# A decoder block's feed-forward stage: a fourth unit of seven block products, and weight sums moved to transfers within SBUF

## The chip, the cores and the metric

The kernel runs on one core of a Trainium2 chip. The metric is device time in microseconds of one execution. Three runs of the kernel before gave 487.75, 488.26 and 488.61 us (median 488.26). One more execution was profiled; all views below come from it.

## The reference, cut to what matters

A block of a decoder with 256 tokens and 1024 channels: a gated linear recurrence and a block attention in parallel, joined, projected, and then a dense feed-forward network (FFN). The change touches only the FFN:

```python
h2 = rmsnorm(x, ffn_norm_g[l])
x = x + (jax.nn.silu(h2 @ w_ffn_gate[l]) * (h2 @ w_ffn_up[l])) @ w_ffn_down[l]
```

`w_ffn_gate` and `w_ffn_up` are 1024 x 2816, `w_ffn_down` is 2816 x 1024, all float32.

## The kernel before, in words

**Precision by splits.** Every float32 operand of a matmul is split in two: a high half, rounded to the fp32r type by a copy on ScalarE (ACT), and a low half, the difference, by a subtraction on VectorE (DVE). A product is then three matmuls: high x high, high x low, low x high. So each 1 MB piece of weights (128 partitions x 2048 elements) costs one ACT cast (L793, `h:` in the order below), one DVE subtraction (L797, `l:`), and matmuls on TensorE (PE, `M:`). Raw weights, high halves and low halves have three buffers each.

**The FFN.** The 2816 columns are cut in three: the first 768 are computed as feature blocks (a, b, e, f: features on partitions, 256 tokens along the row), 1024 columns "B" and 1024 columns "A" as token blocks (tokens on partitions). Gate columns of B and A, and up columns of A, are each a *unit* of seven block products (`scheme`, L919): the product of a 2 x 2 block of tokens and channels by a 2 x 2 block of channels and columns takes seven block products in place of eight, at the price of sums of weight blocks and of token blocks beforehand and of result blocks afterwards. The units are GB, GA and UA. A unit loads four quarters w11, w21, w12, w22 of 1 MB (`L:GBw11` and so on), each into a tile of its own tag, and forms four weight sums in place: 5 (w11 with w12), 6 (w11 with w22), 7 (w12 with w22) and 4 (w21 with w11). A sum is a DVE addition (`S:`, L928) or a transfer that adds while it writes (`A:`, L933, issued by GpSimd, POOL). Product 1 uses w11 as loaded, so sum 5 may only be written once product 1's split has read w11; sum 6 follows the split of 5, and so on. `f:` folds a result block into another on DVE (L968), `c:` copies one from PSUM on ACT (L965), `s:` is the silu, `x:` the product of up and gate.

The up columns of B are computed plainly by `tok` (L971): four pieces v0 to v3, each 1 MB of weights and 24 matmuls of 512 columns. Results of B and A are transposed by PE (`turn`, L997, names `tB..`, `tA..`) and split, and eleven `down` steps (d0 to d10, L1034) of 24 matmuls each multiply them by `w_down` into four PSUM banks.

**The order.** Each step is a closure in a table `todo`; the list `ORDER` (L1069), which a planner has written, says in which order the closures are issued. Each engine works off its own instructions in that order: PE the `M:`, ACT `h: c: s: i:`, DVE `l: S: f: x: k:`, the SP queue the loads `L:`, POOL the `A:`. An instruction that has to wait holds up all behind it on its engine. `SEQ` (L1065) is PE's order in short, `BY_DMA` names the sums that go by transfer, `tags` gives the tiles of each unit's quarters, and `fixed` its PSUM banks. A tile with a tag is free again when the last reader of what was there is done.

Of the kernel before, what the change touches and what calls it, by code (L numbers as in the profile page):

```python
# [11 lines left out]
OP = mybir.AluOpType  # L12
AX = mybir.AxisListType

P = 128
S = 256
D = 1024
KT = D // P
# [9 lines left out]
def tile_hgrn2_moba_block(ctx: ExitStack, tc: tile.TileContext, xm, xw, table, runs,  # L28
                          w_in, w_hg, w_at, w_out, w_gate, w_up, w_down, out):
    nc = tc.nc  # L30
# [7 lines left out]
    def pw(name="pw"):  # L38
        return psum.tile([P, 512], F32, name=name, tag="pw", bufs=4)
# [11 lines left out]
    def part(pair, k, m):  # L51
        return pair[k // 4][:, k % 4, m, :]
# [83 lines left out]
    for kt in range(KT):  # L136
        n0 = 0 if kt == 0 else NV
        t = big.tile([P, NX + D - n0], F32, name=f"xw{kt}", tag=("T3", "T4", "T5", "T1", "T7", "T8", "T9", "T11")[kt])
# [29 lines left out]
    for kt in range(KT):  # L168
        i = kt % 2
# [34 lines left out]
    for j in range(7):  # L204
        c = 1 << j
        n = 64 // c
        for tb in range(2):
            m = mask[:, j, tb, :].rearrange("p (n c) -> p n c", c=c)
# [70 lines left out]
    for half in range(2):  # L279
        ps = F0 if half == 0 else feat_block(w_in, 1024 + half * 512, XT, cut=2 - half)  # L280
        for j in range(2):
            h = half * 4 + j * 2
# [44 lines left out]
    for half in range(2):  # L327
        ps = feat_block(w_in, half * 512, XT)
        for j in range(2):
            h = half * 4 + j * 2  # L330
# [7 lines left out]
    A = big.tile([P, 2, H, P], F32, name="A", tag="T5")  # L338
# [321 lines left out]
    turn_a, b1, turn_h, b3 = pa("turn"), pa("b1"), ph("turn"), ph("b3")  # L660
# [76 lines left out]
    for half in range(2):  # L737
        hs = slice(half * 512, (half + 1) * 512)
        ps = tok_block(w_hg, half * 512, oT)
        for tb in range(2):  # L740
# [6 lines left out]
            ts = slice(tb * P, (tb + 1) * P)  # L747
# [36 lines left out]
    def rows(w, k0, n, c0, cw):  # L784
        return w[k0 * P:(k0 + n) * P, c0:c0 + cw].rearrange("(k p) c -> p k c", p=P)

    todo = {}
# [13 lines left out]
    def chunk(name, src, shape):  # L801
        t = {}

        def load():
            t["raw"] = wp.tile([P] + shape, F32, name="wraw")
            nc.sync.dma_start(t["raw"], src)

        todo["L:" + name] = load
        halve(name, lambda: t["raw"], shape, t)
        return t  # L810
# [85 lines left out]
    class Unit:  # L896
# [13 lines left out]
        def src(self, ij):  # L910
            i, j = int(ij[0]) - 1, int(ij[1]) - 1
            return rows(self.weights, 4 * i, 4, self.c0 + j * 512, 512)
# [6 lines left out]
    def scheme(u):  # L919

        q, banks = u.q, {}

        def load(ij):
            u.w[ij] = big.tile([P, 4, 512], F32, name="W" + ij, tag=dict(zip(("11", "21", "12", "22"), tags[u.name]))[ij])
            nc.sync.dma_start(u.w[ij], u.src(ij))

        def plus(a, b):
            nc.vector.tensor_add(u.w[a], u.w[a], u.w[b])  # L928

        for ij in ("11", "21", "12", "22"):  # L930
            todo[f"L:{u.name}w{ij}"] = lambda ij=ij: load(ij)
        def onto(a, src):
            nc.gpsimd.dma_start(u.w[a], src(), accum_op=OP.add)  # L933

        for k, a, other in (("5", "11", "12"), ("6", "11", "22"), ("7", "12", "22"), ("4", "21", "11")):
            if u.name + k in BY_DMA:
                src = (lambda: u.w["11"][:]) if k == "4" else (lambda other=other: u.src(other))
                todo[f"A:{u.name}{k}"] = lambda a=a, src=src: onto(a, src)
            else:
                todo[f"S:{u.name}{k}"] = lambda a=a, other=other: plus(a, other)  # L940

        def mm(k, t):
            b = {"2": 1, "5": 2, "3": 2}.get(k, 0)
            if k in "125":
                banks[b] = late_bank(fixed[u.name][b]) if u.name in fixed else (pa, ph, pa)[b]()
            act = tokens(*{"1": (0, 0), "2": (0, 1), "4": (1, 1)}[k], x2T) if k in "124" else \
                summed({"5": 0, "6": 1, "7": 2, "3": 3}[k], sums2)
            product(banks[b], act, (t["hi"], t["lo"]), k in "125")

        def through(k, i, j):  # L950
            src = banks[0] if k == "4" else q(i, j)
            if u.gate is None:
                nc.scalar.activation(q(i, j), src, AF.Silu, scale=(r2, r2n)[j if k != "4" else 0][:, i:i + 1])
            elif k in "37":
                nc.vector.scalar_tensor_tensor(q(i, j), src, -1.0, u.gate.q(i, j), op0=OP.mult, op1=OP.mult)
            else:
                nc.vector.tensor_mul(q(i, j), src, u.gate.q(i, j))

        for k, ij in {"1": "11", "2": "21", "5": "11", "6": "11", "7": "12", "3": "22", "4": "21"}.items():
            t = {}  # L960
            name = u.name + k
            halve(name, lambda ij=ij: u.w[ij], [4, 512], t)
            todo["M:" + name] = lambda k=k, t=t: mm(k, t)
        for k, b, i, j in (("1", 0, 0, 0), ("5", 2, 1, 1), ("6", 0, 0, 1)):
            todo["c:" + u.name + k] = lambda b=b, i=i, j=j: nc.scalar.copy(q(i, j), banks[b])  # L965
        for k, b, i, j in (("2", 1, 0, 0), ("3", 2, 0, 1), ("7", 0, 1, 1), ("4", 0, 1, 0)):
            if k != "4":
                todo["f:" + u.name + k] = lambda b=b, i=i, j=j: nc.vector.tensor_add(q(i, j), q(i, j), banks[b])  # L968
            todo[("x:" if u.gate else "s:") + u.name + k] = lambda k=k, i=i, j=j: through(k, i, j)

    def tok(name, j, k0):  # L971

        t = chunk(name, rows(w_up, k0, 4, FB * P + j * 512, 512), [4, 512])
        u = units["UB"]

        def mm():
            if k0 == 0:
                u.ps[j] = [pw(), pw()]
            for i in range(4):
                for tb in range(2):  # L980
                    ts = slice(tb * P, (tb + 1) * P)
                    for m, w in ((0, t["hi"]), (0, t["lo"]), (1, t["hi"])):
                        nc.tensor.matmul(u.ps[j][tb], part(x2T, k0 + i, m)[:, ts], w[:, i, :],  # L983
                                         start=(k0 + i == 0 and m == 0 and w is t["hi"]),
                                         stop=(k0 + i == KT - 1 and m == 1))

        def take(i):
            nc.scalar.copy(u.q(i, j), u.ps[j][i])

        todo["M:" + name] = mm  # L990
        if k0:
            for i in range(2):
                todo[f"c:{name}{i}"] = lambda i=i: take(i)
                k = {(0, 0): "2", (0, 1): "3", (1, 1): "7", (1, 0): "4"}[i, j]
                todo["x:B" + k] = lambda i=i: nc.vector.tensor_mul(u.q(i, j), u.q(i, j), units["GB"].q(i, j))

    def turn(name):  # L997

# [35 lines left out]
    def down(n, f0):  # L1034
# [28 lines left out]
        todo["M:" + name] = mm  # L1063

    SEQ = """  # L1065
        a0 a1 GB1 b0 b1 GB2 e v0 v1 GB5 GB6 GB3 GB7 v2 GB4 v3 tB10 f d0 tB11 tB01 tB00 GA1 GA2 d1 GA5 d2 GA6
        GA3 GA7 d3 GA4 UA1 UA2 d4 UA5 d5 UA6 UA3 UA7 tA001 tA010 d6 tA110 UA4 d7 tA101 d8 d9 d10
    """.split()
    ORDER = """  # L1069
        L:b1 M:a0 L:GBw21 M:a1 L:e h:b0 C0 C1 L:GBw12 Ch0 l:b0 c:a10 h:b1 M:GB1 L:v0 f:a10 c:a11 f:a11 M:b0 h:GB2  # L1070
        L:GBw22 l:b1 s:a10 s:a11 c:GB1 l:GB2 L:v1 S:GB5 M:b1 h:e l:e A:GB7 Cl0 c:b10 L:v2 f:b10 M:GB2 h:v0 C3 c:b11
        l:v0 M:e h:v1 f:b11 L:v3 i:b10 l:v1 i:b11 C2 L:f M:v0 k:b10 h:GB5 k:b11 Ch1 l:GB5 c:e0 S:GB6 M:v1 Cl1 h:GB6
        f:e0 l:GB6 s:e0 M:GB5 h:GB3 S:GB4 c:v11 l:GB3 L:GAw21 M:GB6 h:GB7 c:GB5 l:GB7 M:GB3 L:GAw11 h:v2 c:GB6 l:v2
        M:GB7 h:GB4 L:GAw12 c:v10 l:GB4 M:v2 h:v3 L:d0 f:GB7 l:v3 s:GB7 L:GAw22 f:GB2 f:GB3 M:GB4 h:f L:d1 s:GB2 l:f
        M:v3 s:GB4 h:d0 x:B4 L:d2 s:GB3 l:d0 x:B2 L:d3 M:tB10 c:v30 M:f c:v31 i:tB10 x:B7 h:GA1 x:B3 k:tB10 l:GA1
        S:GA5 M:d0 c:f0 h:GA2 f:f0 A:GA7 l:GA2 i:f0 M:tB11 h:d1 k:f0 M:tB01 M:tB00 M:GA1 i:tB11 i:tB01 k:tB11 i:tB00
        l:d1 M:GA2 h:GA5 L:d4 c:GA1 l:GA5 M:d1 h:d2 l:d2 k:tB01 L:d5 S:GA6 M:GA5 S:GA4 h:GA6 M:d2 h:GA3 l:GA6
        L:UAw21 c:GA5 l:GA3 M:GA6 h:GA7 k:tB00 L:UAw11 f:GA2 s:GA2 l:GA7 M:GA3 h:d3 L:UAw12 c:GA6 l:d3 M:GA7 h:GA4
        L:d6 l:GA4 M:d3 h:UA1 f:GA7 L:UAw22 l:UA1 s:GA7 S:UA5 M:GA4 h:UA2 f:GA3 A:UA7 s:GA3 l:UA2 M:UA1 h:d4 s:GA4
        l:d4 M:UA2 h:UA5 L:d7 c:UA1 l:UA5 M:d4 h:d5 l:d5 S:UA6 L:d8 M:UA5 f:UA2 h:UA6 x:UA2 M:d5 c:UA5 l:UA6 h:UA3  # L1080
        l:UA3 S:UA4 M:UA6 h:UA7 l:UA7 M:UA3 h:d6 c:UA6 l:d6 M:UA7 h:UA4 f:UA3 L:d9 x:UA3 M:tA001 h:d7 f:UA7 M:tA010
        M:d6 x:UA7 l:UA4 i:tA010 i:tA001 k:tA010 k:tA001 l:d7 M:tA110 M:UA4 i:tA110 L:d10 h:d8 k:tA110 l:d8 M:d7
        h:d9 x:UA4 l:d9 M:tA101 M:d8 i:tA101 h:d10 k:tA101 l:d10 M:d9 M:d10
    """.split()
    BY_DMA = ("GA7", "GB7", "UA7")
    late, acc, units = {}, [], {}
    tags = {"GB": ("T10", "T9", "T11", "T8"), "GA": ("T8", "T10", "T11", "T9"), "UA": ("T9", "T8", "T11", "T10")}
    fixed = {"GA": (0, 1, 2), "UA": (3, 1, 2)}
    sums2 = token_sums2()
    for name in ("GB", "UB", "GA", "UA"):  # L1090
        units[name] = Unit(name)
# [70 lines left out]
```

## Time and profile before

| | us |
|---|---|
| median of three runs | 488.26 |
| profiled execution | 488.07 |
| its span, first to last instruction | 486.4 |
| PE busy | 481.6 |
| VectorE busy | 398.5 |
| ScalarE busy | 308.1 |
| GpSimd busy | 28.7 |
| FFN, from its first feature block (304.8) to the last matmul's end | 178 |

The granted TensorE clock was 0.999 of full speed over the span. In the rows of the profile an instruction is "line engine operation written<-read"; "x12" counts instructions, and in brackets stands the idle time ahead of the instruction with what ended it. PE's matmuls overlap, so their distance from start to start is what they cost, not their duration.

### The profile page before, as it was taken

What the parts mean: (1) busy time and instruction counts of PE and PEld (TensorE: products, weight loads), DVE (VectorE), ACT (ScalarE), POOL (GpSimd) and SP (SyncE); (2) the same over time, 40 slices, a digit from 0 to 9 for tenths busy, and PEclk for the clock granted to TensorE, in tenths of its full rate; (3) what the DMA queues carried; (4) which work ended last, traced back from release to release, by engine and by line L of the source; (5) the groups of instructions that cost most, each with busy time, mean ns of one, the idle gap of its engine ahead of it and who ended that gap; (6) DMA issues with size and microseconds to landing.
All of it is one profiled execution on the core that took longest, in us unless ns stands there. A gap on an engine that the chain in (4) does not pass through costs nothing.

```text
span 486.4 us, 6399 instructions
## 1 busy us (share of the span) xinstructions
PE 481.6 (99%) x2538; PEld 403.2 (83%) x2538; DVE 398.5 (82%) x406; ACT 308.1 (63%) x400; POOL 28.7 (6%) x62
## 2 busy tenths in 40 slices
PE   9999999999999999999999999999999999999997
PEld 7888888888888888988888888888878888888886
DVE  5769999697779979499987766889997889989853
ACT  5977646767758984876555445874686547656520
POOL 1930220000000000000000000001000100100000
PEclk9999999999999999999999999999999999999999
DMA  8977695724523348508247575778379466780402
GB/s 310 402 245 256 188 298 184 239 88 138 209 88 132 131 139 291 175 12 334 86 174 250 183 244 189 260 259 225 121 271 340 125 170 222 261 245 11 152 21 88
DMA packets 43695, 94.31 MB, mean 194 GB/s; under 512 B 1673, under 2 KB 3977, under 8 KB 43665
## 3 DMA queue, kind: packets, MB, share of 16 engines
q1 hardware_dynamic: 41344, 88.11, 52.2%
q0 software_dynamic: 2320, 5.79, 5.4%
q8 instruction: 20, 0.33, 0.3%
q14 instruction: 11, 0.08, 0.1%
HBM read 92.82 MB, written 1.07 MB: 193 GB/s over the span
## 4 chain that ended last, share of the span: by engine, by line
PE 94%; DVE 3%; issue 2%; ACT 1%; ACTq 0%
PE acc L1043 12%; PE pw L83 10%; PE pw L84 10%; PE pw L85 10%; PE late L642 8%; PE pw L101 6%; PE pw L165 5%; PE b L642 4%; PE pw L844 4%; PE pa L642 2%; PE pw L983 2%; DVE wlo L797 2%; PE pw L100 2%; PE pw L103 2%; PE pw L680 1%
## 5 line engine op out<-in xcount | busy, mean ns | idle before, releaser
L56 DVE TENSOR_TENSOR wlo<-wraw,whi 128x2048 fp32r<-128x2048 f32 (+1 forms) x42 | 91.5, 2187 | 23.0 <-ACT whi L55 22.8
L55 ACT CAST whi<-wraw 128x2048 fp32r<-128x2048 f32 (+1 forms) x42 | 76.6, 1831 | 38.1 <-PE pw L85 19.6
L83 PE MATMUL pw<-whi,XT 128*128 128x512 f32 x144 | 56.9, 395 | 0.0
L85 PE MATMUL pw<-whi,XT 128*128 128x512 f32 x144 | 56.2, 390 | 0.0
L84 PE MATMUL pw<-wlo,XT 128*128 128x512 f32 x144 | 56.1, 390 | 0.0
L797 DVE TENSOR_TENSOR wlo<-wraw,whi 128x2048 fp32r<-128x2048 f32 x21 | 48.1, 2289 | 9.8 <-ACT whi L793 9.6
L793 ACT CAST whi<-W 128x2048 fp32r<-128x2048 f32 x21 | 40.1, 1915 | 25.2 <-DVE W L928 13.1
L797 DVE TENSOR_TENSOR wlo<-W,whi 128x2048 fp32r<-128x2048 f32 x21 | 47.9, 2289 | 6.4 <-ACT whi L793 6.4
L793 ACT CAST whi<-wraw 128x2048 fp32r<-128x2048 f32 x21 | 40.2, 1912 | 19.8 <-PE pw L844 4.9
L101 PE MATMUL pw<-XT,whi 128*128 128x512 f32 x128 | 40.6, 395 | 0.0
L85 PEld LDWEIGHTS pw<-whi,XT 128*128 128x128 f32 x144 | 27.0, 188 | 5.7
L83 PEld LDWEIGHTS pw<-whi,XT 128*128 128x128 f32 x144 | 27.0, 188 | 5.6
L84 PEld LDWEIGHTS pw<-wlo,XT 128*128 128x128 f32 x144 | 27.1, 188 | 5.4
L844 PE MATMUL pw<-x2T,whi 128*128 128x512 f32 x96 | 31.3, 397 | 0.0
L1043 PE MATMUL acc<-whi,hq 128*128 128x512 f32 x92 | 29.1, 390 | 0.0
L928 DVE TENSOR_TENSOR W<-W,W 128x2048 f32<-128x2048 f32 x9 | 20.6, 2287 | 0.1
L1043 PEld LDWEIGHTS acc<-whi,hq 128*128 128x128 f32 x92 | 17.3, 188 | 3.6
L983 PE MATMUL pw<-whi,x2T 128*128 128x512 f32 x64 | 20.2, 389 | 0.0
L101 PEld LDWEIGHTS pw<-XT,whi 128*128 128x128 f32 x128 | 19.8, 189 | 0.2
L1043 PE MATMUL acc<-wlo,hq 128*128 128x512 f32 x46 | 17.9, 390 | 0.0
L100 PE MATMUL pw<-XT,wlo 128*128 128x256 f32 x64 | 17.8, 278 | 0.0
L103 PE MATMUL pw<-XT,wlo 128*128 128x256 f32 x64 | 17.8, 277 | 0.0
(372 smaller groups left out, 1136.7 us busy)
## 6 DMA issues: line engine op xcount, KB each, us to landing
wraw<-w_in SPq DMA_DIRECT2D x26, 1024.0 KB, 5.1
wraw<-w_down SPq DMA_DIRECT2D x11, 1024.0 KB, 5.0
W<-w_gate SPq DMA_DIRECT2D x8, 1024.0 KB, 7.0
wraw<-w_up SPq DMA_DIRECT2D x7, 1024.0 KB, 5.2
wraw<-w_at SPq DMA_DIRECT2D x4, 1024.0 KB, 6.2
W<-w_in SPq DMA_DIRECT2D x4, 1024.0 KB, 5.2
wraw<-w_hg SPq DMA_DIRECT2D x4, 1024.0 KB, 6.8
wraw<-w_out SPq DMA_DIRECT2D x4, 1024.0 KB, 5.3
```

Of the source, the lines that this page charges most:

```text
L55: high = nc.scalar.copy(hi, src)
L56: return high, nc.vector.tensor_sub(lo, src, hi.bitcast(F32))
L83: nc.tensor.matmul(ps[tb], part(act, kt, 0)[:, ts], wh, start=(kt == 0), stop=False)
L84: nc.tensor.matmul(ps[tb], part(act, kt, 0)[:, ts], wl, start=False, stop=False)
L85: nc.tensor.matmul(ps[tb], part(act, kt, 1)[:, ts], wh, start=False, stop=(kt == KT - 1))
L101: nc.tensor.matmul(ps[ct], hi[:, i, cs], both, start=(kt == 0), stop=(kt == KT - 1))
L642: mm = nc.tensor.matmul(bank, act(kt, m), h[:, kt, :], start=(first and kt == 0 and m == 0 and h is hi), stop=(kt == 3 and m == 1), skip_g ...
L793: nc.scalar.copy(t["hi"], raw())
L797: nc.vector.tensor_sub(t["lo"], raw(), t["hi"].bitcast(F32))
L844: nc.tensor.matmul(block["ps", up][ct], t["hi"][:, i, cs], both, start=(kt == 0), stop=(kt == KT - 1))
L983: nc.tensor.matmul(u.ps[j][tb], part(x2T, k0 + i, m)[:, ts], w[:, i, :], start=(k0 + i == 0 and m == 0 and w is t["hi"]), stop=(k0 + i == ...
L1043: nc.tensor.matmul(bank, ACTS[f0 + i](m, ts), w[:, i, c0:c0 + cw], start=(st and i == 0 and m == 0 and w is t["hi"]), stop=(en and i == 1 ...
```

## The change

The up columns of B become a fourth unit of seven products, UB; `tok` goes. Ten of the sixteen weight sums are made by transfers, and these now read the other quarter from SBUF, where the three of before read it from DRAM a second time. Before, the list of order, the tiles and the banks were made for three units; they are made anew. The order of the down steps' features is the same.

```diff
-        def onto(a, src):
-            nc.gpsimd.dma_start(u.w[a], src(), accum_op=OP.add)
...
             if u.name + k in BY_DMA:
-                src = (lambda: u.w["11"][:]) if k == "4" else (lambda other=other: u.src(other))
-                todo[f"A:{u.name}{k}"] = lambda a=a, src=src: onto(a, src)
+                todo[f"A:{u.name}{k}"] = lambda a=a, other=other: nc.gpsimd.dma_start(u.w[a], u.w[other], accum_op=OP.add)
...
-    def tok(name, j, k0):
...
     SEQ = """
-        a0 a1 GB1 b0 b1 GB2 e v0 v1 GB5 GB6 GB3 GB7 v2 GB4 v3 tB10 f d0 tB11 tB01 tB00 GA1 GA2 d1 GA5 d2 GA6
-        GA3 GA7 d3 GA4 UA1 UA2 d4 UA5 d5 UA6 UA3 UA7 tA001 tA010 d6 tA110 UA4 d7 tA101 d8 d9 d10
+        a0 a1 GB1 b0 GB2 b1 GB5 GB6 GB3 GB7 e GB4 f UB1 UB2 d0 UB5 UB6 UB3 UB7 d1 UB4 GA1 tB002 GA2 d2 GA5
+        GA6 tB101 GA3 GA7 d3 tB112 GA4 UA1 UA2 tB012 d4 d5 UA5 UA6 UA3 UA7 d6 tA011 tA113 UA4 tA002 d7 tA102
+        d8 d9 d10
     """.split()
     ORDER = """
...
+        L:GBw12 M:a0 L:GBw21 L:b1 L:e L:GBw22 M:a1 A:GB5 h:b0 C0 C1 Ch0 l:b0 c:a10 L:f h:GB2 M:GB1 f:a10 c:a11 l:GB2
+        s:a10 f:a11 M:b0 h:b1 C3 c:GB1 l:b1 s:a11 M:GB2 C2 h:GB5 L:d0 Cl0 A:GB7 Ch1 l:GB5 M:b1 S:GB6 Cl1 A:GB4 h:GB6
+        f:GB2 M:GB5 h:GB3 l:GB6 c:b10 l:GB3 M:GB6 h:GB7 c:GB5 l:GB7 L:UBw11 M:GB3 c:GB6 L:UBw21 h:e f:b10 L:UBw12
...
+        k:b10 c:e0 l:UB1 M:f h:UB2 f:e0 i:b11 s:GB4 S:UB5 s:e0 s:GB3 l:UB2 A:UB7 M:UB1 h:d0 k:b11 c:f0 l:d0 M:UB2
+        h:UB5 L:d3 c:UB1 l:UB5 M:d0 S:UB6 f:f0 A:UB4 h:UB6 f:UB2 M:UB5 h:UB3 l:UB6 i:f0 l:UB3 M:UB6 c:UB5 h:UB7
...
+        L:UAw11 M:tB101 h:d3 L:UAw21 M:GA3 L:UAw12 i:tB101 l:d3 c:GA6 M:GA7 h:GA4 k:tB101 L:d6 s:GA2 l:GA4 M:d3
+        h:UA1 f:GA7 L:UAw22 f:GA3 s:GA7 l:UA1 s:GA3 A:UA5 M:tB112 h:UA2 M:GA4 i:tB112 l:UA2 M:UA1 h:d4 k:tB112 s:GA4
+        l:d4 M:UA2 h:d5 L:d7 l:d5 M:tB012 M:d4 A:UA7 i:tB012 h:UA5 k:tB012 L:d8 c:UA1 l:UA5 S:UA6 M:d5 f:UA2 A:UA4
+        h:UA6 x:UA2 l:UA6 M:UA5 h:UA3 l:UA3 M:UA6 c:UA5 h:UA7 l:UA7 M:UA3 h:d6 c:UA6 l:d6 M:UA7 h:UA4 f:UA3 L:d9
...
     """.split()
-    BY_DMA = ("GA7", "GB7", "UA7")
+    BY_DMA = ("GA4", "GA7", "GB4", "GB5", "GB7", "UA4", "UA5", "UA7", "UB4", "UB7")
     late, acc, units = {}, [], {}
-    tags = {"GB": ("T10", "T9", "T11", "T8"), "GA": ("T8", "T10", "T11", "T9"), "UA": ("T9", "T8", "T11", "T10")}
-    fixed = {"GA": (0, 1, 2), "UA": (3, 1, 2)}
+    tags = {"GB": ("T10", "T9", "T11", "T8"), "UB": ("T8", "T10", "T11", "T9"),
+            "GA": ("T9", "T8", "T11", "T10"), "UA": ("T10", "T9", "T11", "T8")}
+    fixed = {"UB": (0, 1, 2), "GA": (3, 1, 2), "UA": (0, 1, 2)}
```

More of the change, by code (lines that the diff above doesn't have):

```diff
@@ L969, in scheme @@
             todo[("x:" if u.gate else "s:") + u.name + k] = lambda k=k, i=i, j=j: through(k, i, j)
-    def tok(name, j, k0):
[L973 to L995, printed above, removed]
     def turn(name):
@@ L1065, in tile_hgrn2_moba_block @@
     SEQ = """
-        a0 a1 GB1 b0 b1 GB2 e v0 v1 GB5 GB6 GB3 GB7 v2 GB4 v3 tB10 f d0 tB11 tB01 tB00 GA1 GA2 d1 GA5 d2 GA6
-        GA3 GA7 d3 GA4 UA1 UA2 d4 UA5 d5 UA6 UA3 UA7 tA001 tA010 d6 tA110 UA4 d7 tA101 d8 d9 d10
+        a0 a1 GB1 b0 GB2 b1 GB5 GB6 GB3 GB7 e GB4 f UB1 UB2 d0 UB5 UB6 UB3 UB7 d1 UB4 GA1 tB002 GA2 d2 GA5
+        GA6 tB101 GA3 GA7 d3 tB112 GA4 UA1 UA2 tB012 d4 d5 UA5 UA6 UA3 UA7 d6 tA011 tA113 UA4 tA002 d7 tA102
+        d8 d9 d10
     """.split()
     ORDER = """
-        L:b1 M:a0 L:GBw21 M:a1 L:e h:b0 C0 C1 L:GBw12 Ch0 l:b0 c:a10 h:b1 M:GB1 L:v0 f:a10 c:a11 f:a11 M:b0 h:GB2
@@ L1071, in tile_hgrn2_moba_block @@
[L1071 to L1080, printed above, removed]
@@ L1081, in tile_hgrn2_moba_block @@
-        l:UA3 S:UA4 M:UA6 h:UA7 l:UA7 M:UA3 h:d6 c:UA6 l:d6 M:UA7 h:UA4 f:UA3 L:d9 x:UA3 M:tA001 h:d7 f:UA7 M:tA010
-        M:d6 x:UA7 l:UA4 i:tA010 i:tA001 k:tA010 k:tA001 l:d7 M:tA110 M:UA4 i:tA110 L:d10 h:d8 k:tA110 l:d8 M:d7
-        h:d9 x:UA4 l:d9 M:tA101 M:d8 i:tA101 h:d10 k:tA101 l:d10 M:d9 M:d10
+        L:GBw12 M:a0 L:GBw21 L:b1 L:e L:GBw22 M:a1 A:GB5 h:b0 C0 C1 Ch0 l:b0 c:a10 L:f h:GB2 M:GB1 f:a10 c:a11 l:GB2
+        s:a10 f:a11 M:b0 h:b1 C3 c:GB1 l:b1 s:a11 M:GB2 C2 h:GB5 L:d0 Cl0 A:GB7 Ch1 l:GB5 M:b1 S:GB6 Cl1 A:GB4 h:GB6
@@ new lines, in tile_hgrn2_moba_block @@
+        f:GB2 M:GB5 h:GB3 l:GB6 c:b10 l:GB3 M:GB6 h:GB7 c:GB5 l:GB7 L:UBw11 M:GB3 c:GB6 L:UBw21 h:e f:b10 L:UBw12
+        c:b11 M:GB7 l:e h:GB4 i:b10 l:GB4 L:d1 M:e h:f f:GB7 s:GB2 L:UBw22 l:f s:GB7 f:b11 L:d2 M:GB4 h:UB1 f:GB3
+        k:b10 c:e0 l:UB1 M:f h:UB2 f:e0 i:b11 s:GB4 S:UB5 s:e0 s:GB3 l:UB2 A:UB7 M:UB1 h:d0 k:b11 c:f0 l:d0 M:UB2
+        h:UB5 L:d3 c:UB1 l:UB5 M:d0 S:UB6 f:f0 A:UB4 h:UB6 f:UB2 M:UB5 h:UB3 l:UB6 i:f0 l:UB3 M:UB6 c:UB5 h:UB7
+        L:GAw11 l:UB7 M:UB3 c:UB6 L:GAw21 h:d1 k:f0 L:GAw12 M:UB7 l:d1 h:UB4 l:UB4 L:d4 M:d1 h:GA1 f:UB7 L:GAw22
@@ new lines, in tile_hgrn2_moba_block @@
+        l:GA1 f:UB3 x:UB2 M:UB4 h:GA2 x:UB3 S:GA5 M:GA1 h:d2 l:GA2 A:GA7 l:d2 M:tB002 h:GA5 M:GA2 i:tB002 l:GA5 L:d5
+        M:d2 S:GA6 k:tB002 A:GA4 h:GA6 x:UB7 x:UB4 c:GA1 M:GA5 l:GA6 h:GA3 f:GA2 M:GA6 h:GA7 l:GA3 c:GA5 l:GA7
+        L:UAw11 M:tB101 h:d3 L:UAw21 M:GA3 L:UAw12 i:tB101 l:d3 c:GA6 M:GA7 h:GA4 k:tB101 L:d6 s:GA2 l:GA4 M:d3
+        h:UA1 f:GA7 L:UAw22 f:GA3 s:GA7 l:UA1 s:GA3 A:UA5 M:tB112 h:UA2 M:GA4 i:tB112 l:UA2 M:UA1 h:d4 k:tB112 s:GA4
+        l:d4 M:UA2 h:d5 L:d7 l:d5 M:tB012 M:d4 A:UA7 i:tB012 h:UA5 k:tB012 L:d8 c:UA1 l:UA5 S:UA6 M:d5 f:UA2 A:UA4
@@ L1084, in tile_hgrn2_moba_block @@
+        h:UA6 x:UA2 l:UA6 M:UA5 h:UA3 l:UA3 M:UA6 c:UA5 h:UA7 l:UA7 M:UA3 h:d6 c:UA6 l:d6 M:UA7 h:UA4 f:UA3 L:d9
+        x:UA3 M:d6 h:d7 f:UA7 x:UA7 l:UA4 l:d7 M:tA011 M:tA113 L:d10 i:tA011 M:UA4 i:tA113 k:tA011 h:d8 k:tA113
+        M:tA002 x:UA4 M:d7 i:tA002 h:d9 k:tA002 l:d8 l:d9 M:tA102 M:d8 i:tA102 h:d10 k:tA102 l:d10 M:d9 M:d10
     """.split()
-    BY_DMA = ("GA7", "GB7", "UA7")
+    BY_DMA = ("GA4", "GA7", "GB4", "GB5", "GB7", "UA4", "UA5", "UA7", "UB4", "UB7")
     late, acc, units = {}, [], {}
-    tags = {"GB": ("T10", "T9", "T11", "T8"), "GA": ("T8", "T10", "T11", "T9"), "UA": ("T9", "T8", "T11", "T10")}
```

## The prediction

> **What bounds the kernel now.** I read the page first, then the chain of waits from 300 us on, then the timelines of PE, DVE and POOL around its one hole, then the groups and the DMA rows.
>
> ```profile
> span 486.4 us, 6399 instructions
> PE 481.6 (99%) x2538; PEld 403.2 (83%) x2538; DVE 398.5 (82%) x406; ACT 308.1 (63%) x400; POOL 28.7 (6%) x62
> ...
> PE 94%; DVE 3%; issue 2%; ACT 1%; ACTq 0%
> ```
>
> The profiled execution took 488.07 us: 486.4 of span and 1.67 around it. PE carries 94% of the chain that ended last. A busy PE need not be at its peak, so the pitch of the matmuls matters:
>
> ```profile
> 307.77 0.47 PE pw L844 x2
> ...
> 308.47 0.47 PE pw L844 x2
> ...
> 317.42 2.72 PE pa L642 x12
> ...
> 362.12 5.44 PE pw L983 x24
> ```
>
> A step of the token products (L983, 24 matmuls) takes 5.44 us and a block product (L642, 12 matmuls) 2.72: both 0.227 us per matmul, without a gap. The feature blocks a, b, e, f repeat four matmuls (two wide, two half) every 0.70 us, so each of their 32-matmul steps takes 8 x 0.70 = 5.60. From 305 us on PE runs at these pitches but for one place:
>
> ```profile
> 355.74 0.47 PE L642 MATMUL pa<-whi,C2h 128*128 128x512 f32 x1
> 356.62 0.50 PE L642 MATMUL pa<-wlo,C2h 128*128 128x512 f32 x1 [0.41 <-DVE wlo L797]
> ...
> 361.96 0.39 PE L983 MATMUL pw<-whi,x2T 128*128 128x512 f32 x1
> ```
>
> At 355.74 product GB3 begins; 24 matmuls later (GB3, GB7) v2 should begin at 355.74 + 5.44 = 361.18 and begins at 361.96. The hole of 0.78 us is DVE's: GB3's low half came late. DVE at that place:
>
> ```profile
> 352.08 2.28 DVE L928 TENSOR_TENSOR W<-W,W 128x2048 f32<-128x2048 f32 x1
> 354.28 4.49 DVE L797 TENSOR_TENSOR wlo<-W,whi 128x2048 fp32r<-128x2048 f32 x2
> ```
>
> The weight sum S:GB4 (L928) stands right ahead of GB3's split (L797). So the FFN is PE's sum plus one DVE hole.
>
> **The change, part by part.**
>
> *The seven products.* v0 to v3 are 4 x 5.44 = 21.76 us of PE; UB's seven products are 7 x 2.72 = 19.04. PE does 2.72 us less. Transposes (four of B, four of A), the other products and the eleven downs are the same in number. All of it lies on PE, hence on the path: **-2.72**.
>
> *DVE and ACT.*
>
> ```profile
> L797 DVE TENSOR_TENSOR wlo<-W,whi 128x2048 fp32r<-128x2048 f32 x21 | 47.9, 2289 | 6.4 <-ACT whi L793 6.4
> L928 DVE TENSOR_TENSOR W<-W,W 128x2048 f32<-128x2048 f32 x9 | 20.6, 2287 | 0.1
> ...
> L968 DVE TENSOR_TENSOR q<-q,late 128x512 f32<-128x512 f32 x6 | 4.1, 681 | 0.0
> ```
>
> ```profile
> L793 ACT CAST whi<-W 128x2048 fp32r<-128x2048 f32 x21 | 40.1, 1915 | 25.2 <-DVE W L928 13.1
> ```
>
> ```profile
> 300.00:470.00 170.00, 169.59 (x811) 141.35 (x810) 146.83 (x115) 107.66 (x101) 3.93 (x3) 1.00 0.61 196
> ```
>
> Seven splits replace four: three more on DVE (3 x 2.29) and ACT (3 x 1.92). UB's three folds (as L968) add 3 x 0.68 on DVE. Each unit of seven products has four weight sums. Before, three units have twelve, three by transfer and nine on DVE; after, four units have sixteen, ten by transfer and six on DVE (GB6, UB5, UB6, GA5, GA6, UA6): -3 x 2.29. DVE comes out 6.87 + 2.04 - 6.87 = 2.0 us longer, 149 of about 167 us; ACT some 5 us longer, 113. Neither becomes the bound as a sum, so this is priced at nothing, covered by PE's 2.7 to 5.6 us steps. Where the cover is thin I follow the queue.
>
> *The hole at GB3.* S:GB4 leaves DVE and becomes a transfer. Rows for the small pieces, and the start of the queue:
>
> ```profile
> L825 DVE TENSOR_TENSOR C2l<-C,C2h 128x1024 fp32r<-128x1024 f32 x2 | 2.4, 1219 | 0.0
> ...
> L871 DVE TENSOR_TENSOR zt<-zt,R 128x512 f32<-128x512 f32 x3 | 2.1, 692 | 0.1
> ...
> L819 DVE TENSOR_TENSOR C<-x2f 128x512 f32<-128x512 f32 x1 | 0.7, 685 | 0.0
> ```
>
> ```profile
> 309.59 2.29 DVE L797 TENSOR_TENSOR wlo<-W,whi 128x2048 fp32r<-128x2048 f32 x1 [1.12 <-ACT whi L793]
> ...
> 316.20 0.75 DVE L867 TENSOR_TENSOR zt<-pw,zt 128x256 f32<-128x256 f32 x2
> ```
>
> Back to back, instructions follow 0.08 sooner than they last (352.08 and 354.28 above: 2.20). In the new order DVE has, from the end of GB1's split to the end of GB7's, eight 2.2 us pieces (splits of b0, GB2, b1, GB5, GB6, GB3, GB7 and S:GB6), the C pieces (two of 1.2, four of 0.65), two folds of a (1.4 each), R and its parts (1.0) and GB2's fold (0.65): 17.6 + 5.0 + 2.8 + 1.7 = 27.1 us. 311.9 + 27.1 = 339.0. PE's new order from 320.14 (end of GB1) is b0 to 325.74, GB2 328.46, b1 334.06, GB5 336.78, GB6 339.50, GB3 342.22, then GB7. So GB7's split has 3.2 us to spare as a sum, and the hole goes: **-0.78**. What is late next is a chain across engines.
>
> *Chain GB5 to GB6.* There are three high-half buffers, so h:GB5 waits until b0's product ends, 325.74. Then h:GB5 1.92, l:GB5 2.29, S:GB6 2.29 (it writes what l:GB5 read), h:GB6 1.92, l:GB6 2.29: 10.7, ending 336.5. GB6's second matmul needs it at 336.78 + 0.23 = 337.0. It fits by 0.5. The same five steps in UB run from the end of UB1 beside UB2 + d0 + UB5 = 2.72 + 5.44 + 2.72 and 0.23 = 11.1 us; there two folds (1.4 for f0, 0.68) stand between S:UB6 and l:UB6, 0.2 longer than h:UB6, and crossings of queues add some 0.1: 11.0 to 11.3. Taken as a hole of **+0.2** at UB6.
>
> *Ten adding transfers.* Before has three, each from DRAM; SBUF to SBUF is not in the trace. The nearest rows:
>
> ```profile
> W<-w_gate POOLq DMA_DIRECT2D x2, 1024.0 KB, 9.2
> ...
> x<-xm POOLq DMA_DIRECT2D x1, 1024.0 KB, 5.2
> W<-w_up POOLq DMA_DIRECT2D x1, 1024.0 KB, 8.4
> ```
>
> ```profile
> 383.84 1.30 POOL L933 DMA_DIRECT2D W<-w_gate  x1 [54.18 <-DVE fl L867]
> ```
>
> ```profile
> 384.61 2.28 DVE L797 TENSOR_TENSOR wlo<-W,whi 128x2048 fp32r<-128x2048 f32 x1
> ...
> 390.32 2.28 DVE L797 TENSOR_TENSOR wlo<-wraw,whi 128x2048 fp32r<-128x2048 f32 x1
> ```
>
> ```profile
> 388.00:389.00 1.00, 1.00 (x8) 0.91 (x7) 0.00 (x0) 1.00 (x1) 0.00 (x0) 1.00 1.09 201
> ...
> 390.00:391.00 1.00, 1.00 (x6) 0.82 (x5) 1.00 (x2) 0.65 (x2) 0.00 (x0) 1.00 1.16 213
> ```
>
> ```profile
> 432.00:433.00 1.00, 1.00 (x6) 0.81 (x5) 1.00 (x1) 0.00 (x0) 0.00 (x0) 1.00 1.02 422
> ```
>
> The columns that matter are the last two, DMA share and GB/s. An adding transfer, alone, fills all 16 engines (1.09 to 1.16) and moves 201 to 213 GB/s, where plain loads move 422. So 1 MB holds the engines 5.1 us instead of 2.6, and lands 8.4 us after issue without company, against 5.2 for a plain one from the same queue. Bounds for the SBUF source: below, the plain 5.2 (no HBM behind it); above, three passes where the row's halving stands for two, 7.7 us on the engines and 11.0 to landing. I take 8.5, the adding rows; most of what they do is the same. POOL issues them in 1.30 each and has nothing else to do here, and DVE's splits keep their 2.28 beside the issue (384.61) and the transfer (390.32).
>
> Now they are in a chain: A:GB7 writes w12, which A:GB5 reads, so it is issued only when A:GB5 has landed, and A:GB4 needs S:GB6. The moved loads matter too.
>
> ```profile
> 304.95 0.37 SPq L925 DMA_DIRECT2D W<-w_gate  x1
> ...
> 316.20 0.50 SPq L925 DMA_DIRECT2D W<-w_gate  x1
> ```
>
> w21 waits for a tile until 304.95; b1, e and w22 now queue on SP behind it (w22 went at 316.20), and f follows at about 316. That is 5 MB plain (13.0 us) and A:GB5 (issued 311.9): first data at 307.0 (of the 5.2 us that a plain one takes 2.6 are data, about 2 lie ahead of them); on engines that then never idle, 307.0 + 13.0 + 5.1 = 325.1, landed 325.5; without company 320.4. Needed: 325.74, free until 326.2. A:GB7: 325.6 + 8.5 and d0's 2.6 beside it = 336.7; h:GB7's buffer comes free at 336.78, its split ends at 341.0 for a need of 342.4.
>
> ```profile
> 375.73 0.44 PE turn L1005 x4
> ```
>
> UA: h:UA1's buffer comes free with the end of GA7's product; 1.92, 2.29 and about 1 for the folds that stand ahead on DVE make 5.2 until l:UA1 ends and A:UA5 can go; PE has d3, GA4, UA1, UA2, d4, d5, UA5 and two transposes before UA6's low half, 28.3 us from GA7's end; 5.2 + 8.5 + 10.8 = 24.5, and UA's last quarter shares some 1.8: 2.0 to spare. At 8.5 all ten are covered, so priced at nothing; if the cover goes, below.
>
> **Sum.** 488.07 - 2.72 - 0.78 + 0.2 = 484.8. The median of the three runs before, 488.26, is 0.2 above the profiled one, so 485.0.
>
> **Rivals.**
>
> *Late transfers (slower).* If each transfer holds the engines 7.7 us, all that is covered above is late. A:GB5 lands at 328.4 or later, GB6 loses over 2. A:UA5 comes at least 2.6 later against 2.0 to spare, and once product UA5 waits for its own split, UA6 waits for S, h and l behind it, 6.5 less 2.72, another 3.8. Behind ACT's waiting h:UA5 stand c:UA1 and the next casts, and PE behind those. With GB7, GB4 and GA each losing about 1: 2.4 + 0.6 + 3.8 + 3 = 9.8, **494.6**. It decides from about 9.8 us to landing (6.4 on the engines, 165 GB/s): GB6 loses 1 to 2 there and UA6 begins to. For it: destination, source and result all lie in SBUF. Against it: the halving in the rows can be two reads for each write, of which only one was SBUF's; then the other's place need not matter. [...] Chance 0.18.
>
> *Cover partly gone.* Transfers land 1 us later, or sharing is worse than counted: GB6 loses 0.7, UB6 and GA another 0.8: **486.5**. Chance 0.13.
>
> *No gain.* DVE at 149 of 167 us has no room in the stages with sums (UB, GA), and late splits open three or four holes of 0.8 like GB3's: 484.8 + 3.2, **488.0**. For it the hole of before; against it the 3 us that the queue has to spare. Chance 0.08.
>
> **How the numbers follow.** The forecast has 0.61, with a range of its own from 484.2 (the UB6 hole absent, and 0.5 of shape) to 485.7. About 0.2%, 1 us, is what the measurement can tell. Faster: 0.61 + 0.13 and little of the third, 0.74; same 0.07; slower 0.19. The range goes to 490, past the first two rivals and the beginning of the slow one, and leaves that one out.
>
> **What would show it.** Right: 2.7 us less PE busy in the chain, no matmul waiting for DVE for more than 0.3 us, adding transfers near 8.5 us, A:GB5 landed before b0's product ends. Wrong: PE or its loads waiting at GB6, UA5 or UA6; rows of L793 waiting for the DMA; adding transfers under 165 GB/s; or DVE's L797 and L928 longer than 2.29 beside ten transfers.

## The result and the profile after

The changed kernel takes 485.2 us (median of 8 runs, 484.79 to 487.27); the kernel before, beside it, 488.08 (8 runs, 487.69 to 488.71). The ratio is 0.9944, with a 95% interval of 0.9931 to 0.9958: faster by 2.9 us. The profiled execution took 485.24 us, its span is 483.4; before, 488.07 and 486.4.

The page of the changed kernel: the span, the engines' busy times and, from its fourth part, the chain by engine.

```profile
span 483.4 us, 6406 instructions
PE 479.1 (99%) x2526; PEld 401.0 (83%) x2526; DVE 400.2 (83%) x409; ACT 312.7 (65%) x402; POOL 33.3 (7%) x69
...
PE 99%; DVE 0%; issue 0%
```

PE has 12 matmuls less (2538 to 2526). VectorE is busy 1.7 us longer and ScalarE 4.6, where 2.0 and about 5 were worked out. DVE's 3% of the chain and ACT's 1% are gone: the end is now set by PE alone. The chain of waits of the changed kernel, PE's work in order of time:

```profile
334.03 11.01 PE pa L642 x48
...
358.91 5.44 PE late L642 x24
364.35 5.44 PE acc L1013 x24
369.79 11.17 PE late L642 x48
```

The first line is GB5, GB6, GB3 and GB7, 48 matmuls in 11.01 us where the pitch gives 10.88; the hole of 0.78 that GB3 had is not there. Then UB1 and UB2, d0, and UB5, UB6, UB3, UB7 in 11.17: here the hole at UB6 is. The two matmuls around it, from PE's timeline:

```profile
372.35 0.39 PE L642 MATMUL late<-whi,C2h 128*128 128x512 f32 x1
372.69 0.50 PE L642 MATMUL late<-wlo,C2h 128*128 128x512 f32 x1
373.03 0.40 PE L642 MATMUL late<-whi,C2l 128*128 128x512 f32 x1
```

Twice 0.34 from start to start in place of 0.227: 0.23 us, for the +0.2 of the prediction. GpSimd's timeline, the ten adding transfers at their issue, and the page's line of their time to landing:

```profile
312.21 0.97 POOL L934 DMA_DIRECT2D W<-W  x1 [68.86 <-DVE r L218]
325.33 0.88 POOL L934 DMA_DIRECT2D W<-W  x1 [12.15 <-DMA W<-w_gate]
332.92 0.85 POOL L934 DMA_DIRECT2D W<-W  x1 [6.71 <-issue]
...
417.61 0.86 POOL L934 DMA_DIRECT2D W<-W  x1 [17.73 <-DMA W<-w_up]
428.24 0.86 POOL L934 DMA_DIRECT2D W<-W  x1 [9.78 <-DMA W<-W]
```

```profile
W<-W POOLq DMA_DIRECT2D x10, 1024.0 KB, 9.5
```

One by one they land 11.5, 9.0, 7.7, 8.8, 7.8, 8.4, 10.0, 10.3, 11.9 and 10.0 us after issue. The ones of 7.7 (issued at 332.92) and 7.8 (issued at 368.81) had the DMA engines to themselves for nearly all of their way. GB5's, with four loads beside it, landed at 312.2 + 11.5 = 323.7. What waited for it, h:GB5, and for UA5's, h:UA5, from ScalarE's timeline:

```profile
325.82 1.92 ACT L793 CAST whi<-W 128x2048 fp32r<-128x2048 f32 x1 [1.13 <-issue]
...
428.04 1.91 ACT L793 CAST whi<-W 128x2048 fp32r<-128x2048 f32 x1 [0.97 <-DMA W<-W]
```

h:GB5 starts when its buffer comes free at 325.8, not when the transfer lands; h:UA5 does wait for its transfer, 0.97 us, and PE loses nothing by it.

### The profile page after: what moved, and what is told of

It is laid out like the page before. It is cut to its first block, busy times and chain, and to the rows that moved or that the text cites. A ratio compares the mean times of both kernels' runs of the same rounds, so it can differ in the third digit from the quotient of the medians.

```text
span 483.4 us, 6406 instructions
## 1 busy us (share of the span) xinstructions
PE 479.1 (99%) x2526; PEld 401.0 (83%) x2526; DVE 400.2 (83%) x409; ACT 312.7 (65%) x402; POOL 33.3 (7%) x69
## 4 chain that ended last, share of the span: by engine, by line
PE 99%; DVE 0%; issue 0%
PE acc L1013 12%; PE late L642 12%; PE pw L83 10%; PE pw L85 10%; PE pw L84 10%; PE pw L101 6%; PE pw L165 5%; PE pw L844 5%; PE b L642 4%; PE pa L642 3%; PE pw L103 2%; PE pw L100 2%; PE pw L680 2%; PE pw L681 2%; PE pw L679 1%; PE pw L843 1%
## 5 line engine op out<-in xcount | busy, mean ns | idle before, releaser
L793 ACT CAST whi<-W 128x2048 fp32r<-128x2048 f32 x28 | 53.4, 1915 | 33.5 <-DVE W L928 16.7
L797 DVE TENSOR_TENSOR wlo<-W,whi 128x2048 fp32r<-128x2048 f32 x28 | 63.8, 2290 | 10.7 <-ACT whi L793 10.2
L797 DVE TENSOR_TENSOR wlo<-wraw,whi 128x2048 fp32r<-128x2048 f32 x17 | 38.8, 2289 | 5.1 <-ACT whi L793 4.9
L793 ACT CAST whi<-wraw 128x2048 fp32r<-128x2048 f32 x17 | 32.6, 1915 | 11.2 <-PE pw L85 5.8
L642 PE MATMUL late<-whi,x2T 128*128 128x512 f32 x72 | 23.3, 394 | 0.0
L934 POOL DMA_DIRECT2D W<-W x10 | 8.7, 869 | 183.9 <-DVE r L218 68.9
L642 PE MATMUL late<-whi,C2h 128*128 128x512 f32 x48 | 18.9, 393 | 0.0
L642 PE MATMUL late<-wlo,C2h 128*128 128x512 f32 x48 | 18.8, 393 | 0.0
L642 PE MATMUL late<-whi,C2l 128*128 128x512 f32 x48 | 18.7, 390 | 0.0
```

What stands on the lines that cost most here:

```text
L642: mm = nc.tensor.matmul(bank, act(kt, m), h[:, kt, :], start=(first and kt == 0 and m == 0 and h is hi), stop=(kt == 3 and m == 1), skip_g ...
L793: nc.scalar.copy(t["hi"], raw())
L797: nc.vector.tensor_sub(t["lo"], raw(), t["hi"].bitcast(F32))
```

## The experiments

Each changes the kernel named in its heading; "before" runs stood beside every one of them on the same chip.

### One product more (changed kernel)

```diff
             product(banks[b], act, (t["hi"], t["lo"]), k in "125")
+            if u.name + k == "UB3":
+                product(late_bank(3), act, (t["hi"], t["lo"]), True)
```

> The changed kernel with UB's product 3 done twice, the second time into a free bank that nobody reads: 12 matmuls more on PE (2.72 us), nothing more on any other engine. If PE's sum sets the time, as the prediction has it: 485.2 + 2.7 = 487.9. If the gain came from relief of VectorE or from the transfers, and PE has slack in UB: under 486.2, with the extra product hidden beside waits.

488.17 us, against 488.24 of before (ratio 0.9995, 0.9986 to 1.0004): the gain is gone. In the chain of waits UB5, UB6, UB3 and UB7 with their 12 matmuls more:

```profile
370.24 13.89 PE late L642 x60
```

13.89 against 11.17 is 2.72, all of it on the path. PE has no slack in UB, and the products are nearly all of the gain. By the prediction's sum, what the two holes change should still leave this run 0.6 us under before. Its median is 0.07 under, with an interval from 0.7 under to 0.2 over: that difference is at the edge of what the medians can tell.

### GB4's sum by a transfer (kernel before)

```diff
-... c:e0 S:GB6 M:v1 ... M:GB5 h:GB3 S:GB4 c:v11 l:GB3 ...
+... c:e0 S:GB6 M:v1 ... M:GB5 h:GB3 A:GB4 c:v11 l:GB3 ...
...
-    BY_DMA = ("GA7", "GB7", "UA7")
+    BY_DMA = ("GA7", "GB7", "UA7", "GB4")
```

> The kernel before, with one sum (GB4) made by an adding transfer in place of VectorE, and nothing else. If the hole ahead of GB3 is VectorE's late low half and nothing stands behind it: 488.1 - 0.75 = 487.3, and no matmul waits near 356 us. If the hole only moves to the next wait (v2 or GB4): 487.9 to 488.3.

487.58 us (ratio 0.9986, 0.9977 to 0.9995): 0.66 less than the 488.24 beside it. VectorE's timeline now has GB3's split, the one that ended at 356.57 in the kernel before, here:

```profile
349.88 2.29 DVE L797 TENSOR_TENSOR wlo<-W,whi 128x2048 fp32r<-128x2048 f32 x1
352.48 2.29 DVE L797 TENSOR_TENSOR wlo<-W,whi 128x2048 fp32r<-128x2048 f32 x1 [0.31 <-ACT whi L793]
```

It ends at 354.77, and GB3's first matmuls follow at the pitch but for some 0.1; nothing stands behind the hole. The interval allows 0.2 to 1.1 us, the hole of 0.78 lies in it.

### The source of the transfers, both ways

In the kernel before, the three transfers read SBUF:

```diff
-                src = (lambda: u.w["11"][:]) if k == "4" else (lambda other=other: u.src(other))
+                src = lambda other=other: u.w[other][:]
```

> The kernel before, its three adding transfers reading the other quarter from SBUF and not from DRAM, nothing else. The prediction's theory: those three are hidden, so 488.1 within 0.3; the transfers land in 7.7 to 9 us. Rival (3 MB less of HBM reads brings loads sooner, or a third pass through SBUF brings the sums later): under 487.5, or over 488.7.

488.03 us (ratio 0.9998, 0.9989 to 1.0007): no difference. The three, with a median a little under the 7.7 to 9 us expected:

```profile
W<-W POOLq DMA_DIRECT2D x3, 1024.0 KB, 7.6
```

In the changed kernel, six of ten read DRAM:

```diff
-... lambda a=a, other=other: nc.gpsimd.dma_start(u.w[a], u.w[other], accum_op=OP.add)
+... lambda k=k, a=a, other=other: nc.gpsimd.dma_start(u.w[a], u.w[other] if k == "4" else u.src(other), accum_op=OP.add)
```

> The changed kernel, its sums 5 and 7 (six of the ten transfers) reading the other quarter from DRAM again; the sums 4 read SBUF as they must. If the price of a transfer is the same from either source and all are covered: 485.2 to 485.7. If the source in SBUF is what lets ten of them fit (6 MB more of HBM reads delay the loads): over 486.5, with waits at GB6 or UA6.

485.4 us (ratio 0.9942, 0.9930 to 0.9955), the changed kernel's time. GB5's and GB7's transfers no longer depend on each other and go out together at 312.20. The DMA view has the three from `w_gate`, and ScalarE's timeline shows what GB5's did to h:GB5:

```profile
W<-w_gate POOLq DMA_DIRECT2D x3, 1024.0 KB, 13.6
```

```profile
325.88 1.92 ACT L793 CAST whi<-W 128x2048 fp32r<-128x2048 f32 x1 [1.20 <-DMA W<-w_gate]
```

GB5's landed after 13.6 us, at 325.8, just as the buffer came free: at the edge, and no hole. So the source is not what lets ten transfers fit. From DRAM, in the two places where it ran alone in the kernel before (GA7 and UA7), the transfer took 8.5 and 8.4 us; from SBUF, the two that ran nearly alone in the changed kernel (issued at 332.92 and 368.81) took 7.7 and 7.8. By the DMA view the packets of these hold the 16 engines for 5.1 and 5.2 us against 6.1 and 6.2 (79.2% of 6.4 us and 51.8% of 10, against 51.2% of 12 and 44.0% of 14). They are also larger (144 of them against 528), so the source isn't the only difference. GpSimd needs about 0.86 us instead of 1.30 to issue it; nothing in the end hangs on any of this.

### Stores ahead of every transfer (changed kernel)

```diff
...
+        def late_add(u, k, a, other):
+            extra = dram.tile([P, 4, 512], F32, name="x" + u.name + k)
+            nc.gpsimd.dma_start(extra, u.w[other][:, 0:4, :])
+            nc.gpsimd.dma_start(u.w[a], u.w[other], accum_op=OP.add)
```

(half of it: `[P, 2, 512]` and `0:2`)

> The changed kernel; ahead of each of the ten adding transfers GpSimd issues a plain store of 0.5 MB of the same quarter to DRAM, which nobody reads. Each sum's data then hold the engines about 1.3 us longer, which is where the prediction put the edge (6.4 us on the engines). Its theory: GB6 loses 1 to 2, UA6 begins to lose: 487 to 490.5. If the transfers have much more room than that: 485.2 to 486.

> The same with a store of 1 MB ahead of each of the ten: 2.6 us more on the engines for each sum, the price of the prediction's slow rival. Its theory: GB6, UA5 and UA6, and some of GB7, GB4 and GA late, 490 to 500, with 494.6 as the sum of its steps. If late transfers are harmless: under 488.

491.18 us with 0.5 MB (ten runs, 488.24 to 492.55; ratio 1.0048, 1.0030 to 1.0067) and 497.93 with 1 MB (ratio 1.0196, 1.0179 to 1.0213). Slower than before in both, as the slow rival has it; the first lies a little above its expected range of 487 to 490.5. Its ten runs differ by the clock: the four with a mean clock of 1.0 took 488.24 to 491.08, the six with 0.996 to 0.999 took 490.19 to 492.55. The places are another matter. PE's and ScalarE's timelines with 0.5 MB, the waits at UA6 and h:UA5:

```profile
441.68 0.50 PE L642 MATMUL late<-whi,C2h 128*128 128x512 f32 x1 [0.82 <-ACT whi L793]
444.00 0.50 PE L642 MATMUL late<-wlo,C2h 128*128 128x512 f32 x1 [1.83 <-DVE wlo L797]
```

```profile
433.05 1.91 ACT L793 CAST whi<-W 128x2048 fp32r<-128x2048 f32 x1 [5.21 <-DMA W<-W]
```

h:UA5 waits 5.2 us, and UA6 loses twice, for its high half and for its low one, as worked out. UB6's hole grows as well, from 0.23 to 0.70. But GB6, expected first, loses nothing. GpSimd's timeline with 1 MB says why:

```profile
300.23 0.59 POOL L940 DMA_DIRECT2D xGB<-W  x1 [56.51 <-DMA W<-w_gate]
312.57 0.91 POOL L941 DMA_DIRECT2D W<-W  x1 [11.75 <-DVE r L218]
```

The store for GB5 reads w12, which had landed long before, so it was over by the time the transfer went: the dose missed this one. GB5's transfer needed a run of its own. Nor is the dose as clean elsewhere as it was meant to be, since the stores hold up the loads too: with 0.5 MB UA5's transfer, which waits for a load of `w_up`, goes out at 420.77 in place of 417.61, and lands 5.0 us later for 1.3 us of store. These two runs show where late transfers hurt, not how late one transfer may be.

### GB5's transfer alone late (changed kernel)

```diff
...
+            if u.name + k == "GB5":
+                extra = dram.tile([P, 16], F32, name="extra")
+                nc.gpsimd.dma_start(extra, u.w["22"][:, 0, 0:16])
...
```

> The changed kernel; ahead of the adding transfer of GB5 alone GpSimd stores 8 KB of w22, which nobody reads, so that it must wait until w22 has landed (about 318 to 319 us; by itself the transfer is issued at 312.2). It then lands at about 327.5 to 328.5. The prediction's chain: it may land until 326.2 unpunished, later ones move GB6's low half by as much. So GB6 opens a hole of 1.3 to 2.3 us ahead of its second matmul and nothing else is late: 486.5 to 487.6. If the chain has more room than that or GB6 isn't first: 485.2 with no hole at GB6.

488.29 us (twelve runs, 486.97 to 489.87; ratio 0.9996, 0.9984 to 1.0008): 3.1 more than the changed kernel, more than expected. The profiled execution took 489.47. GpSimd issued the transfer at 321.18. On ScalarE, h:GB5:

```profile
328.49 1.91 ACT L793 CAST whi<-W 128x2048 fp32r<-128x2048 f32 x1 [3.29 <-DMA W<-W]
```

and on PE, the first matmuls of GB6 and some behind them:

```profile
337.13 0.49 PE L642 MATMUL pa<-whi,C2h 128*128 128x512 f32 x1
339.46 0.50 PE L642 MATMUL pa<-wlo,C2h 128*128 128x512 f32 x1 [1.83 <-DVE wlo L797]
...
341.08 0.63 PE L642 MATMUL pa<-whi,C2h 128*128 128x512 f32 x1
341.50 0.63 PE L642 MATMUL pa<-wlo,C2h 128*128 128x512 f32 x1
```

The place and the size are the chain's: from h:GB5's start at 328.49, h, l, S, h and l end at 339.4, and GB6's second matmul starts 2.33 after its first instead of 0.23, a hole of 2.1. What the prediction lacked stands below it: matmuls at 0.43 us from start to start. The windows of the same execution, with the granted clock third from the end:

```profile
339.00:340.00 1.00, 0.54 (x2) 0.48 (x3) 1.00 (x2) 1.00 (x3) 0.00 (x0) 1.00 0.79 164
340.00:341.00 1.00, 1.00 (x4) 0.81 (x3) 1.00 (x1) 1.00 (x1) 0.00 (x0) 0.64 1.30 262
341.00:342.00 1.00, 1.00 (x4) 0.73 (x3) 1.00 (x2) 0.69 (x2) 0.00 (x0) 0.50 0.67 131
342.00:343.00 1.00, 1.00 (x4) 0.80 (x3) 1.00 (x1) 0.00 (x0) 0.00 (x0) 0.50 0.45 68
343.00:344.00 1.00, 1.00 (x4) 0.75 (x4) 1.00 (x2) 0.13 (x1) 0.00 (x0) 0.66 0.80 209
```

After the hole the clock is halved for about 3.4 us, 1.6 us more lost. Not in every run: the twelve have mean clocks of 0.995 or 0.996 in five (488.51 to 489.87) and 0.999 or 1.0 in seven (486.97 to 488.52). The second group is what the hole alone costs: its median, 487.31, is 2.1 above the changed kernel.

### Sums back on VectorE (changed kernel)

```diff
-    BY_DMA = ("GA4", "GA7", "GB4", "GB5", "GB7", "UA4", "UA5", "UA7", "UB4", "UB7")
+    BY_DMA = ()
```

(with `S:` for `A:` in the order; for the second kernel the four sums 7 stay `A:`)

> The changed kernel with all sixteen weight sums on VectorE, each at the same place of the order. VectorE gets 10 x 2.2 = 22 us more beside the FFN's 165 us, 149 + 22 = 171: it becomes the bound. By that 6 us of it at the least can't be hidden, and the sums bunch: 491 to 498. If VectorE had room and the transfers weren't needed: 485 to 487.

> The changed kernel with only the four sums 7 by transfer (as before had three) and twelve sums on VectorE, same order: 6 x 2.2 = 13 us more, 162 of 165 us. If the moved sums are what makes room for the fourth unit: 487 to 492, slower than the changed kernel and about as slow as before. If only the products count: 485 to 486.

500.88 us with none by transfer (ratio 1.0256, 1.0239 to 1.0273) and 492.5 with the four sums 7 (ratio 1.0089, 1.0074 to 1.0104). Both lie over their expected ranges, the first by 2.9 us, the second by 0.5, and in the profiles of both the clock halves after holes (matmuls at 0.43 us from start to start in place of 0.227), which no expectation had. VectorE and PE in the second, at GB6:

```profile
333.92 2.28 DVE L928 TENSOR_TENSOR W<-W,W 128x2048 f32<-128x2048 f32 x1
336.12 0.68 DVE L964 TENSOR_TENSOR q<-q,ph 128x512 f32<-128x512 f32 x1
336.72 6.69 DVE L797 TENSOR_TENSOR wlo<-W,whi 128x2048 fp32r<-128x2048 f32 x3
```

```profile
339.06 0.50 PE L642 MATMUL pa<-wlo,C2h 128*128 128x512 f32 x1 [1.82 <-DVE wlo L797]
```

S:GB4 (333.92) stands in front of GB6's split (336.72), the pattern of the hole in the kernel before. UB6 and GA6 wait in the same way, 2.15 and 1.35 us from PE's starts, and after UB6's hole the clock halves as above (0.50 from 379 to 381); after GB6's, of 2.0 us, it does not (0.23 from start to start). So in this order the fourth unit only pays with sums taken off VectorE: with the products but twelve sums on VectorE the kernel is 4 us slower than before. Orders made anew for so many sums on VectorE were not tried.

## Why the prediction was right

**Products, -2.72.** Right: 2.72 in the chain of the run with one product more, and its time is back at that of before.

**The hole at GB3, -0.78.** Right: gone in the profile after; taken out alone it is worth 0.66 in the median.

**The hole at UB6, +0.2.** Right in place and size (0.23), the size in part by luck. The 0.2 was put on the folds that stand ahead of UB6's split. ScalarE's and VectorE's timelines have the cast h:UB6, the last fold and the split:

```profile
368.39 3.73 ACT L793 CAST whi<-W 128x2048 fp32r<-128x2048 f32 x2 [4.28 <-DVE W L928]
```

```profile
369.59 0.68 DVE L964 TENSOR_TENSOR q<-q,late 128x512 f32<-128x512 f32 x1
370.34 6.93 DVE L797 TENSOR_TENSOR wlo<-W,whi 128x2048 fp32r<-128x2048 f32 x3
```

The folds end at 370.27, and the cast, the first of the two in its row, at 370.30, so the folds add nothing. The five steps take the 10.7 us worked out, and the hand-overs between the engines add some 0.5, where 0.1 was allowed. No run took the hole out.

**Ten adding transfers at nothing.** Right, though sized loosely. Nearly alone they take 7.7 and 7.8 us where 8.5 was assumed; GB5's landed at 323.7 for 325.5, GB7's at 334.3 for 336.7, UA5's at 427.9 for a forecast of about 427.4 (GA7's product ended at 411.9; 5.2, 8.5 and some 1.8 of company behind that). Two of the starts were ended by another wait than the one worked out. In GpSimd's timeline GB7's transfer, at 325.33, waits for the load of w22 and not for GB5's transfer, which had landed at 323.7; that its start agrees with the 325.6 of the prediction is luck. UA5's, at 417.61, waits for a load of `w_up`, 0.8 us after the split l:UA1 had ended. What the slow rival rested on, 7.7 us on the engines for three passes through SBUF, isn't there: the SBUF source is no slower (7.7 and 7.8 us to landing against 8.4 and 8.5), and its packets hold the engines for 5.1 and 5.2 us. The edge, 9.8 us to landing, was meant for a transfer without company, and no run tests it alone; in company five of the ten take about 10 us or more and cost nothing. What decides is each transfer's landing against its own need, and there the chain was right: GB5 late by itself opens the hole at GB6, of the size worked out.

**The slow rival's sum.** 494.6 was its price, with 497.93 measured at that dose; but it had GB6 pay first, where the dose missed GB5, and it had no term for the clock.

**The sum.** -3.3 was forecast and -2.8 measured in the profile (488.07 to 485.24), -2.9 in the medians. The matmuls' starts from the FFN's first one on show where part of the rest went. Slips of 0.08 us and more against the pitch add up to 1.67 before and 1.23 after. GB3's hole leaves (0.77) and UB6's comes (0.23), which would make 1.13. Most of the other 0.1 is at the transposes, which the prediction took as the same because their number is the same. Their grouping is not: before they stand in five groups, now in seven, and in both traces the second matmul behind every group starts 0.09 to 0.10 late. Here is the first group of the changed kernel:

```profile
391.68 0.60 PE L975 MATMUL late<-ident,q 128*128 128x128 f32 x4
392.04 0.48 PE L642 MATMUL late<-whi,x2T 128*128 128x512 f32 x1
392.35 0.40 PE L642 MATMUL late<-wlo,x2T 128*128 128x512 f32 x1
```

From 392.04 to 392.35 is 0.31 in place of 0.227. Two groups more make nearly 0.2, and one slip of 0.08 from before is gone. No run changes the grouping alone, so this cause is read from the traces and not tested. Another 0.1 lies outside the span (1.7 us around it before, 1.8 after). What remains, some 0.2, is mostly in slips under 0.08. It is as much as one execution differs from the next; it isn't settled.

No variant run here beats the changed kernel; the one with DRAM sources equals it.

## What to carry to other kernels

When one engine sets the end, a change is worth what it takes from that engine, as long as every step that feeds it keeps a positive slack: follow each new wait as a chain from the buffer that frees to the matmul that needs it, and compare with the work of the busy engine over the same stretch. Count the groups of small steps on that engine as well as the steps: here each group of transposes came with a loss of 0.1. Moving work to transfers is then judged by landing against need, not by how long a transfer takes. In the profiled execution with GB5 late a hole cost more than itself: 2.1 us, and 1.6 more with the clock at half behind it.

## What the runs showed of the hardware

*The clock fell after a short hole, in some executions.* A pause of 1.8 us in PE's work (2.1 us lost) was followed by half clock (0.50) for about 3.4 us in the profiled execution with GB5 late; five of its twelve runs have a mean clock of 0.995 or 0.996, the other seven 0.999 or 1.0. A hole of 2.15 us at UB6 in the run with the four sums 7 was followed by half clock as well, again for about 3.4 us. It did not always happen: after the hole of 2.0 us at GB6 in that same execution, and after those of 1.0 and 2.1 us at UA6 with 0.5 MB of stores, the matmuls came at 0.23 us from start to start, the pitch of the full clock.

*An adding transfer from SBUF cost no more than one from DRAM, as the two are issued here.* Alone or nearly so, 7.7 and 7.8 us against 8.4 and 8.5 for 1 MB, and about 0.86 us of GpSimd's time to issue against 1.30.

*A store put ahead of GB5's transfer on GpSimd's queue went out 12 us before it.* With 1 MB the store was issued at 300.23, since its own source was ready, and the transfer, which waited for something else, at 312.57, against 312.21 without a store.
